# Preparing a weight pair's first blocks ahead of the preceding W1 chunk, and every later run head by seven products, in an fp32 MLP on Trainium2

## The chip, the cores and the metric

The kernel runs on one core of a Trainium2 chip. A core has a matrix engine (PE in the profile, its weight loads PEld), a vector engine (DVE), a scalar engine (ACT), a general engine (POOL) and a sync engine (SP), which here issues the loads of the weights from HBM. Each engine works through its own queue strictly in order and waits on semaphores of the others. Sums of products stand in PSUM, in eight banks of 128 x 512 fp32; everything else stands in SBUF.

The metric is device time of one run in microseconds, the median of several runs. The profile comes from one further run; its span goes from that run's first instruction to its last.

## The reference

A trunk of two layers over 256 tokens of width 2048. Layer 0 mixes with a gated short convolution, layer 1 with multi-head latent attention; both are followed by the same kind of MLP with a hidden width of 8192, which is where the change is:

```python
def sq_relu_mlp(x, w1, w2):
    return jnp.square(jax.nn.relu(x @ w1)) @ w2

for layer in range(DEPTH):          # DEPTH = 2
    ...
    h = layer_norm(ALPHA * h + mix, ln_g[layer, 0], ln_b[layer, 0])
    h = layer_norm(ALPHA * h + sq_relu_mlp(h, mlp_w1[layer], mlp_w2[layer]),
                   ln_g[layer, 1], ln_b[layer, 1])
```

All inputs are float32, 256 tokens are held as two halves of 128, and the result is float32.

## The kernel before

**Split numbers.** Every fp32 operand is cut into a rounded high part and the rest: `split` (L142) has ACT cast `hi` and DVE subtract `lo = src - hi`. A product is then three matrix multiplications, high x high, high x low and low x high (`dot`, L293). So each weight block costs ACT a cast and DVE a subtraction of its full size, besides its time on PE.

**The weight stream.** All weights come in one list, `stream`, in the order of use. An entry is a *unit* (one 128 x 1024 block; two units make one *chunk*, that is 128 columns of W1), or a *pair* of W2 blocks: *plain* or *fast*. `prepare(i)` (L168) loads the raw blocks of an entry into `raws` (6 buffers of 512 KB), and splits them into `hi`/`lo` tiles of `whl` (8 buffers each). It is a generator in one, two or three stages; `take` (L215) runs these stages ahead of the use, up to `WA` = 8 stages past the entry that it hands out.

**Plain and fast groups.** A pair times the activations of two halves is a 2 x 2 block product. A plain group does it with eight products (`PLAINS`, 24 multiplications on PE) on four blocks as they are. A fast group does it with seven (`FAST`, 21 multiplications), after Strassen's and Winograd's manner, and so needs sums of weight blocks. They are made by DVE in place in the raw blocks: three differences (L193, `minus`, 128 x 512 each), each of which touches what the one before it read or wrote, then the split of the two new blocks T1 and T2 (tiles `hi_t`, `lo_t`), a fourth difference and its split T4 (tile `t4`, one buffer). The sums of activation blocks that a fast group needs are made by `forms` (L660) for every chunk pair.

**Order of the work.** `plan` (L81) makes runs of four groups, in turn for the two halves b of the output's columns (the first run has two groups), and puts one chunk of W1 behind each group from the fourth group on. A chunk (L716) is 16 high and 16 low multiplications into one bank `ps_m`, which `whole` (L333) clears with an ACT copy `t` and a DVE addition `sf`; every second chunk is followed by ReLU and square on ACT (L722, L658), `forms` on DVE and a split into `hc` (ACT) and `ha` (DVE). While groups run, `ps_m` has a single bank, so a chunk starts when the `sf` of the chunk before it is done. In `PLAIN` (L39) the pairs 0 and 1 of both halves are plain, and of half 1 also 4, 8, 12, ... 24, the heads of its later runs: ten plain groups of 56 in each layer.

**Turns.** Seven partial sums stand in seven PSUM banks. When a run ends, `Sums.turn` (L604) copies each bank to SBUF (`spill`, L584) and the other half's sum back into it (`seed`, L588), both on ACT. Behind a plain head the sum of product 1 is swapped once more (L741). A scheduler then places all instructions on their engines' queues, by its own estimates; the queue order is what runs.

Of the kernel before, what the change touches and what calls it, by code (L numbers as in the profile page):

```python
# [31 lines left out]
RAW, WA = 6, 8  # L32
# [3 lines left out]
KEPT = PAIRS - QC // 2  # L36
SLOTS = 10
FIRST = ((0, 2, 4, 8), (0, 4, 8))
PLAIN = ((0, 1), (0, 1, *range(4, KEPT, 4)))  # L39
GROUP = 3  # L40
WARM = 8
WO_G = 3
# [6 lines left out]
def trunk(ctx: ExitStack, tc: tile.TileContext, xT, vecs, w_in, w_out, w_kv, w_q, w_uk, w_uv,  # L49
# [26 lines left out]
    stream = []  # L76
# [4 lines left out]
    def plan():  # L81

        nxt, b, steps, m, count = [0, 0], 0, [], QC, 0
        while min(nxt) < KEPT:
            end = min(nxt[b] + (4 if nxt != [0, 0] else 2), KEPT)
            run = [(b, j, j in PLAIN[b]) for j in range(nxt[b], end)]
            for i, (b, j, plain) in enumerate(run):
# [23 lines left out]
    size = {"unit": 1, "plain": 2, "fast": 3}  # L111
    start = [0]
# [3 lines left out]
    class Banks:  # L116
# [15 lines left out]
        @classmethod  # L132
        def next(cls):
            cls.count += 1
            if cls.only is not None:
                return cls.only
            return cls.more if cls.more is not None and cls.count % 8 >= 4 else pmm

    state = {"made": 0, "next": 0}
    ready = {}  # L140

    def split(hi, lo, src):  # L142

        nc.scalar.copy(hi, src)  # L144
        nc.vector.tensor_tensor(lo, src, hi.bitcast(F32), ALU.subtract)  # L145

    def tiled(w):
        return w.rearrange("p (b c) -> p b c", c=P)

    def parts(i):  # L150
        return tuple(whl.tile([P, 8, P], F32R, tag=t, name=f"{t}{i}") for t in ("hi", "lo"))
# [11 lines left out]
    def load_raw(i, src):  # L163
        raw = raws.tile([P, 1024], F32, tag="raw", name=f"raw{i}")
        nc.sync.dma_start(raw, src)
        return raw

    def prepare(i):  # L168

        kind, *src = stream[i]  # L170
        if kind == "unit":
            raw = load_raw(i, src[0])
            hi, lo = ready[i] = parts(i)
            split(hi, lo, tiled(raw))
            yield
            return
        r1, r2 = (load_raw(f"{i}_{j}", v) for j, v in enumerate(src))

        def finished(r, name):
            w = parts(f"{i}_{name}")  # L180
            split(*w, tiled(r))
            return [[v.rearrange("p b c -> p (b c)")[:, o:o + BW] for v in w] for o in (0, BW)]

        b11, b22, b21, b12 = r1[:, :BW], r1[:, BW:], r2[:, :BW], r2[:, BW:]
        out = {}
        if kind == "plain":
            out["11"], out["22"] = finished(r1, 1)
            yield
            out["21"], out["12"] = finished(r2, 2)
            ready[i] = out  # L190
            yield
            return
        minus = lambda o, x, y: nc.vector.tensor_tensor(o, x, y, ALU.subtract)  # L193
        out["11"], out["22"] = finished(r1, 1)
        minus(b11, b12, b11)
        minus(b12, b12, b22)
        minus(b22, b22, b11)
        yield
        out["T1"], out["T2"] = finished(r1, "t")
        minus(b11, b21, b22)  # L200
        f = state["fast"].tile([P, 2, BW], F32R, tag="t4", name=f"t4_{i}", bufs=1)
        split(f[:, 0, :], f[:, 1, :], b11)
        out["T4"] = [f[:, 0, :], f[:, 1, :]]
        yield
        out["21"], out["T3"] = finished(r2, 2)
        ready[i] = out
        yield

    def all_steps():
        for i in range(2 * GROUP, len(stream)):  # L210
            yield from prepare(i)

    making = all_steps()

    def take(n=2):  # L215

        i = state["next"]
        state["next"] += n
        while state["made"] < min(start[i] + WA, start[-1]):
            next(making)  # L220
            state["made"] += 1
        got = [ready.pop(i + j) for j in range(n)]
        return got

    def psum(name):
        return Banks.next().tile([P, 512], F32, tag="mm", name=name)
# [18 lines left out]
    def mm_like(ps, w, x, n=NC):  # L245

        for h in range(0, NC, n):
            for k in range(h, h + n):
                high(ps, w, k, x[k], k == 0)
            for k in range(h, h + n):  # L250
                low(ps, w, k, x[k], k == NC - 1)
# [22 lines left out]
    def group_of(n):  # L274

        return [(take(), psum("ps_g")) for _ in range(n)]
# [56 lines left out]
    def whole(ps, out):  # L333

        t = tmp.tile([P, T], F32, tag="evac", name="t")
        nc.scalar.copy(t, ps[:, T:])
        nc.vector.tensor_tensor(out, ps[:, :T], t, ALU.add)  # L337
# [174 lines left out]
    for half, cuts in enumerate(FIRST):  # L512
        pieces = [load(2 * u + half, first[:, GROUP * half + u, :], cuts) for u in range(GROUP)]
        for b0, b1 in zip(cuts, cuts[1:]):
            at = slice(8 * half + b0, 8 * half + b1)
# [4 lines left out]
                put_split(xhl[m], xres[:, m, :])  # L520
            for p in pieces:
                next(p)
    state["made"] = 2 * GROUP
    nc.sync.dma_start(vec, vecs)

    zt = array("b", F32R, "z", NC, 2 * T)
# [4 lines left out]
    for m in range(NC):  # L531
# [17 lines left out]
        if m >= NC // 2:  # L549
# [4 lines left out]
    summed(ln, products(NC, z), residual)  # L554

    FAST = (("1", "11", "11"), ("3", "S4", "22"), ("5", "S1", "T1"), ("6", "S2", "T2"),
            ("4", "22", "T4"), ("2", "12", "21"), ("7", "S3", "T3"))
    PLAINS = (("3", "12", "22"), ("1", "22", "22"), ("2", "11", "11"), ("4", "21", "11"),
              ("3", "11", "12"), ("1", "21", "12"), ("2", "12", "21"), ("4", "22", "21"))

# [77 lines left out]
    def mlp(idx, ln, hook, blocks, fast):  # L638
# [8 lines left out]
        def normal():  # L647
            k = next(todo, None)
            if k is not None:
                ln.normal(k, xhl[k])  # L650
# [3 lines left out]
        def pair():  # L654
            return fast.tile([P, 8 * P], F32, tag="sf", name="sf", bufs=2)

        def square(f):
            nc.scalar.activation(f[:, :4 * P], f[:, :4 * P], AF.Square)  # L658

        def forms(f):  # L660

            a21, a11, a12 = (f[:, i * P:(i + 1) * P] for i in (1, 0, 2))
            s1, s2, s4 = (f[:, i * P:(i + 1) * P] for i in (4, 6, 7))
            blocks = f.rearrange("p (a c) -> p a c", c=P)
            nc.vector.tensor_tensor(s1, a21, f[:, 3 * P:4 * P], ALU.add)
            nc.vector.tensor_tensor(blocks[:, 5:7, :], blocks[:, 1:5:3, :], a11.unsqueeze(1).to_broadcast([P, 2, P]),
                                    ALU.subtract)
            nc.vector.tensor_tensor(s4, a12, s2, ALU.subtract)
# [31 lines left out]
        def parts_of(j):  # L700

            i = j % 4
            if j >= 4:
                both = [(one[:, i, c * P:(c + 1) * P], two[:, i, c * P:(c + 1) * P]) for c in range(8)]
            else:
                both = [[t[:, i, (4 * o + c) * P:(4 * o + c + 1) * P] for o in range(2)] for t in (one, two) for c in range(4)]
            return dict(zip(NAMES, both))
# [4 lines left out]
        for at, step in enumerate(steps):  # L712
            if step[0] == "m":
                m = step[1]
                w, ps = take(), psum("ps_m")
                mm_like(ps, w, xhl, 8)  # L716
                if m % 2 == 0:
                    f = pair()
                half = f[:, m % 2 * T:(m % 2 + 1) * T]
                whole(ps, half)  # L720
                if m % 2:
                    nc.scalar.activation(f[:, :4 * P], f[:, :4 * P], AF.Relu)  # L722
                    square(f)
                    j, cols = m // 2, 4 * P
                    if j < KEPT:
                        forms(f)
                        cols = 8 * P
                    split(one[:, j % 4, :cols], two[:, j % 4, :cols], f[:, :cols])
                if m == FF // P - 3:
                    Banks.only = None  # L730
                continue
            _, b, j, plain, first, last = step
            w, = take(1)
            later = [s for s in steps[at + 1:] if s[0] == "group"]
            turns = plain and bool(later) and not later[0][3]
            sums.group(b, w, parts_of(j), plain, last, turns)
            if later:
                if last:
                    sums.turn(later[0][1], later[0][3])
                elif turns:  # L740
                    sums.spill("1")  # L741
                    sums.seed("1", (b, "1"))
            if first and j + 4 >= KEPT and b == 0 and j + 2 >= KEPT:
                folded = sums.fold(1)
            if not later:
                folded = sums.combine(0) + folded
            if count < 4:
                normal()
                normal()
            if hook is not None:  # L750
                hook(count)
            count += 1
# [37 lines left out]
    with tc.tile_pool(name="fast1", bufs=1) as fast:  # L790
        mlp(1, before, prepare_one, to_wide, fast)
# [250 lines left out]
    with tc.tile_pool(name="fast2", bufs=1) as fast:  # L1042
        mlp(3, after, None, to_out, fast)
# [86 lines left out]
```

## Time and profile before

| what | value |
|---|---|
| median of 3 runs | 2031.51 us (2030.67 to 2031.93) |
| the profiled run | 2031.37 us |
| span of its profile | 2029.6 us, 29846 instructions |
| granted PE clock, mean | 0.999 |
| first and last multiplication of a group (`sum`) | 413.9 us and 1945.9 us, with the attention layer between |
| loads | 385 MB, 190 GB/s over the span |

Times in the profile are counted from the span's start. In the timeline view a row has the start, the length, the engine, the line, the operation, the tiles written and read, the shape and how many equal instructions stand in the row; in brackets stands how long the engine was idle before it and who ended the wait. Lengths of two instructions in a row overlap a little, so what an instruction costs its engine is read from start to start. Tile names have no numbers there; in queue order listings they have, and the first number is the entry's place in `stream`.

### The profile page before, as it was taken

How to read it: one execution, taken by the hardware profiler on the slowest of the kernel's cores; microseconds unless marked ns; L12 is line 12 of the kernel's file. 1: busy time of each engine (PE TensorE's matmuls, PEld its weight loads, DVE VectorE, ACT ScalarE, POOL GpSimd, SP SyncE). 2: the span in 40 equal slices, each digit the busy share in tenths (PEclk: the TensorE clock that was granted, in tenths of full speed). 3: DMA queues.
4: the chain of work that ended last, by engine and by line, in shares of the span. 5: the costliest groups of instructions: out<-in, count | busy, mean ns of one | idle time of the engine just before them, and what ended most of it. 6: DMA issues, size and time to landing. Idle time of an engine off the chain costs nothing.

```text
span 2029.6 us, 29846 instructions
## 1 busy us (share of the span) xinstructions
PE 2004.9 (99%) x11088; PEld 1735.4 (86%) x11088; DVE 1729.8 (85%) x2575; ACT 1384.2 (68%) x2071; POOL 2.3 (0%) x21
## 2 busy tenths in 40 slices
PE   9999999999999999999999999999999999999997
PEld 8888888988888888888889998898888888888886
DVE  7667677799999999999988888779899999999996
ACT  6444445577877888777756655568777788787861
POOL 0000000000000000000000000000000000000000
PEclk9999999999999999999999999999999999999999
DMA  9665556455555565555654534655555556556672
GB/s 312 206 190 190 189 189 189 150 183 194 180 207 179 205 207 198 203 174 207 235 189 157 167 124 131 201 168 166 187 189 199 193 207 208 182 196 203 207 231 102
DMA packets 108002, 385.31 MB, mean 190 GB/s; under 512 B 11984, under 2 KB 13392, under 8 KB 107856
## 3 DMA queue, kind: packets, MB, share of 16 engines
q1 hardware_dynamic: 107712, 383.13, 56.6%
q8 instruction: 87, 1.43, 0.3%
q14 instruction: 59, 0.48, 0.1%
q10 hardware_dynamic: 144, 0.26, 0.0%
HBM read 381.25 MB, written 2.10 MB: 189 GB/s over the span
## 4 chain that ended last, share of the span: by engine, by line
PE 61%; DVE 17%; ACT 14%; issue 5%; DMA 2%; DVEq 0%; ACTq 0%; SPq 0%
PE ps_u L230 13%; PE ps_m L230 9%; PE ps_u L234 7%; DVE lo L145 7%; PE ps_m L234 5%; DVE raw L193 4%; ACT hi L144 4%; PE sum L296 3%; PE sum L297 3%; PE sum L295 3%; ACT sums L584 2%; ACT hi_t L144 2%; DVE lo_t L145 2%; ACT sum L588 2%; DMA raw<-in_w_dram 1%
## 5 line engine op out<-in xcount | busy, mean ns | idle before, releaser
L145 DVE TENSOR_TENSOR lo<-raw,hi 128x1024 fp32r<-128x1024 f32 x712 | 850.7, 1219 | 127.8 <-ACT hi L144 51.2
L144 ACT CAST hi<-raw 128x1024 fp32r<-128x1024 f32 x712 | 726.2, 1050 | 261.2 <-PE ps_u L230 158.1
L230 PE MATMUL ps_m<-xhl,hi 128*128 128x512 f32 x1792 | 449.3, 391 | 3.0 <-DVE sf L337 2.2
L230 PEld LDWEIGHTS ps_m<-xhl,hi 128*128 128x128 f32 x1792 | 328.6, 188 | 69.1 <-DVE sf L337 2.8
L234 PEld LDWEIGHTS ps_m<-xhl,lo 128*128 128x128 f32 x1792 | 244.3, 190 | 17.4
L234 PE MATMUL ps_m<-xhl,lo 128*128 128x256 f32 x1792 | 249.7, 282 | 0.0
L296 PE MATMUL sum<-lo,hc 128*128 128x512 f32 x512 | 202.9, 396 | 1.0 <-DVE lo L145 1.0
L295 PE MATMUL sum<-hi,hc 128*128 128x512 f32 x512 | 196.8, 396 | 5.2 <-ACT sum L588 5.1
L193 DVE TENSOR_TENSOR raw<-raw,raw 128x512 f32<-128x512 f32 x276 | 189.3, 686 | 3.0
L297 PE MATMUL sum<-hi,ha 128*128 128x512 f32 x448 | 175.1, 391 | 0.0
L144 ACT CAST hi_t<-raw 128x1024 fp32r<-128x1024 f32 x92 | 96.6, 1050 | 113.5 <-DVE raw L193 113.4
L230 PE MATMUL ps_u<-xhl_a,hi 128*128 128x512 f32 x720 | 172.0, 391 | 0.0
L145 DVE TENSOR_TENSOR lo_t<-raw,hi_t 128x1024 fp32r<-128x1024 f32 x92 | 112.7, 1225 | 68.5 <-ACT hi_t L144 68.5
L230 PEld LDWEIGHTS ps_u<-xhl_a,hi 128*128 128x128 f32 x720 | 132.4, 188 | 25.8
L584 ACT COPY sums<-sum 128x512 f32<-128x512 f32 x204 | 118.0, 583 | 43.3 <-PE sum L297 41.4
L295 PEld LDWEIGHTS sum<-hi,hc 128*128 128x128 f32 x512 | 95.6, 188 | 31.5 <-ACT sum L588 9.4
L296 PEld LDWEIGHTS sum<-lo,hc 128*128 128x128 f32 x512 | 96.5, 189 | 23.5 <-DVE lo L145 8.4
L588 ACT COPY sum<-sums 128x512 f32<-128x512 f32 x186 | 110.0, 593 | 2.7
L297 PEld LDWEIGHTS sum<-hi,ha 128*128 128x128 f32 x448 | 84.3, 188 | 15.9
L234 PEld LDWEIGHTS ps_u<-xhl_a,lo 128*128 128x128 f32 x720 | 92.3, 191 | 3.5
L234 PE MATMUL ps_u<-xhl_a,lo 128*128 128x256 f32 x720 | 93.4, 283 | 0.0
L722 ACT ACTIVATE sf<-sf 128x512 f32<-128x512 f32 x56 | 35.4, 631 | 57.2 <-DVE sf L337 57.2
(240 smaller groups left out, 3285.0 us busy)
## 6 DMA issues: line engine op xcount, KB each, us to landing
raw<-in_w_dram SPq DMA_DIRECT2D x288, 512.0 KB, 4.5
raw<-in_w2f_dram SPq DMA_DIRECT2D x224, 512.0 KB, 5.7
raw<-in_w_in_dram SPq DMA_DIRECT2D x90, 512.0 KB, 4.3
raw<-in_w_out_dram SPq DMA_DIRECT2D x32, 512.0 KB, 4.1
raw<-in_w_o_dram SPq DMA_DIRECT2D x32, 512.0 KB, 3.9
raw<-in_w_kv_dram SPq DMA_DIRECT2D x10, 512.0 KB, 4.3
raw<-in_w_q_dram SPq DMA_DIRECT2D x8, 512.0 KB, 4.0
raw<-in_w_uk_dram SPq DMA_DIRECT2D x8, 512.0 KB, 4.2
```

The costliest lines, as they stand in the source:

```text
L144: nc.scalar.copy(hi, src)
L145: nc.vector.tensor_tensor(lo, src, hi.bitcast(F32), ALU.subtract)
L193: minus = lambda o, x, y: nc.vector.tensor_tensor(o, x, y, ALU.subtract)
L230: nc.tensor.matmul(ps, w[blk // 8][0][:, blk % 8, :], x, start=first, stop=False)
L234: nc.tensor.matmul(ps[:, :T], w[blk // 8][1][:, blk % 8, :], x[:, :T], start=False, stop=last)
L295: nc.tensor.matmul(ps, x[0], w[0], start=first, stop=False, skip_group_check=goes_on)
L296: nc.tensor.matmul(ps, x[0], w[1], start=False, stop=False, skip_group_check=goes_on)
L297: nc.tensor.matmul(ps, x[1], w[0], start=False, stop=last, skip_group_check=goes_on)
L584: nc.scalar.copy(self.slot(self.live.pop(p)), self.bank[p])
L588: nc.scalar.copy(self.bank[p], self.at(key))
L722: nc.scalar.activation(f[:, :4 * P], f[:, :4 * P], AF.Relu)
```

## The change

The change has four parts. `PLAIN` loses the heads of later runs, so six more groups of each layer are fast. The stages of `prepare` are ordered anew: wherever the stream has unit, unit, fast, the pair's first stage (both loads, the first split and three differences) now comes ahead of the two units, and its second and third stages behind them; within these, the split of the second raw block changes places with the fourth difference and T4's split. `take` gets a parameter: at a run's last group only five stages ahead are made instead of eight, so that the turn's copies stand ahead of the casts that follow. Last, `FAST` has the product with T4 as the last of its seven instead of the fifth.

```diff
--- before.py
+++ after.py
@@ -36,7 +36,7 @@
 KEPT = PAIRS - QC // 2
 SLOTS = 10
 FIRST = ((0, 2, 4, 8), (0, 4, 8))
-PLAIN = ((0, 1), (0, 1, *range(4, KEPT, 4)))
+PLAIN = ((0, 1), (0, 1))
 GROUP = 3
 WARM = 8
 WO_G = 3
@@ -198,29 +198,41 @@
         yield
         out["T1"], out["T2"] = finished(r1, "t")
         minus(b11, b21, b22)
+        yield
+        out["21"], out["T3"] = finished(r2, 2)
         f = state["fast"].tile([P, 2, BW], F32R, tag="t4", name=f"t4_{i}", bufs=1)
         split(f[:, 0, :], f[:, 1, :], b11)
         out["T4"] = [f[:, 0, :], f[:, 1, :]]
-        yield
-        out["21"], out["T3"] = finished(r2, 2)
         ready[i] = out
         yield
 
-    def all_steps():
-        for i in range(2 * GROUP, len(stream)):
-            yield from prepare(i)
-
-    making = all_steps()
-
-    def take(n=2):
+    sequence, i = [], 2 * GROUP
+    while i < len(stream):
+        if [k for k, *_ in stream[i:i + 3]] == ["unit", "unit", "fast"]:
+            sequence += [i + 2, i, i + 1, i + 2, i + 2]
+            i += 3
+        else:
+            sequence += [i] * size[stream[i][0]]
+            i += 1
+    making = {}
+    last = {i: at for at, i in enumerate(sequence)}
+
+    def make_up_to(n):
+
+        while state["made"] < min(n, len(sequence)):
+            i = sequence[state["made"]]
+            state["made"] += 1
+            if i not in making:
+                making[i] = prepare(i)
+            next(making[i])
+
+    def take(n=2, ahead=None):
 
         i = state["next"]
         state["next"] += n
-        while state["made"] < min(start[i] + WA, start[-1]):
-            next(making)
-            state["made"] += 1
-        got = [ready.pop(i + j) for j in range(n)]
-        return got
+        mine = max(last.get(j, -1) + 1 for j in range(i, i + n))
+        make_up_to(max(mine, start[i] - 2 * GROUP + (WA if ahead is None else ahead)))
+        return [ready.pop(i + j) for j in range(n)]
 
     def psum(name):
         return Banks.next().tile([P, 512], F32, tag="mm", name=name)
@@ -520,7 +532,6 @@
                 put_split(xhl[m], xres[:, m, :])
             for p in pieces:
                 next(p)
-    state["made"] = 2 * GROUP
     nc.sync.dma_start(vec, vecs)
 
     zt = array("b", F32R, "z", NC, 2 * T)
@@ -554,7 +565,7 @@
     summed(ln, products(NC, z), residual)
 
     FAST = (("1", "11", "11"), ("3", "S4", "22"), ("5", "S1", "T1"), ("6", "S2", "T2"),
-            ("4", "22", "T4"), ("2", "12", "21"), ("7", "S3", "T3"))
+            ("2", "12", "21"), ("7", "S3", "T3"), ("4", "22", "T4"))
     PLAINS = (("3", "12", "22"), ("1", "22", "22"), ("2", "11", "11"), ("4", "21", "11"),
               ("3", "11", "12"), ("1", "21", "12"), ("2", "12", "21"), ("4", "22", "21"))
 
@@ -730,7 +741,7 @@
                     Banks.only = None
                 continue
             _, b, j, plain, first, last = step
-            w, = take(1)
+            w, = take(1, 5 if last else None)
             later = [s for s in steps[at + 1:] if s[0] == "group"]
             turns = plain and bool(later) and not later[0][3]
             sums.group(b, w, parts_of(j), plain, last, turns)
```

**DVE, middle of layer 0's MLP, one fast pair (213) and what is made beside it.** `lo213_1` belongs to the pair's first split, the rows L193 on `raw213` are its differences, `lo213_t` T1 and T2, `lo213_2` the second raw block, `t4_213` T4; `lo211` to `lo215` are units of chunks, `sf` clears a chunk, `ha1` belongs to the activations. Before:

```order
L145 TENSOR_TENSOR lo213_1_6367<-raw213_0_6362,hi213_1_6366 128x1024
L337 TENSOR_TENSOR sf_6406<-ps_m_6373,t_6407 128x256
L193 TENSOR_TENSOR raw213_0_6362<-raw213_1_6364,raw213_0_6362 128x512
L193 TENSOR_TENSOR raw213_1_6364<-raw213_1_6364,raw213_0_6362 128x512
L193 TENSOR_TENSOR raw213_0_6362<-raw213_0_6362 128x512
L145 TENSOR_TENSOR lo213_t_6411<-raw213_0_6362,hi213_t_6410 128x1024
L145 TENSOR_TENSOR lo213_2_6419<-raw213_1_6364,hi213_2_6418 128x1024
L193 TENSOR_TENSOR raw213_0_6362<-raw213_1_6364,raw213_0_6362 128x512
L145 TENSOR_TENSOR lo214_6447<-raw214_6444,hi214_6446 128x1024
L145 TENSOR_TENSOR lo215_6453<-raw215_6450,hi215_6452 128x1024
L145 TENSOR_TENSOR t4_213_6415<-raw213_0_6362,t4_213_6415 128x512
L145 TENSOR_TENSOR lo216_1_6461<-raw216_0_6456,hi216_1_6460 128x1024
```

With the change (line numbers are those of the changed file, where L349 is the old L337):

```order
L145 TENSOR_TENSOR lo213_1_6367<-raw213_0_6362,hi213_1_6366 128x1024
L145 TENSOR_TENSOR ha1_4154<-sf_6225,hc1_3517 128x1024
L193 TENSOR_TENSOR raw213_0_6362<-raw213_1_6364,raw213_0_6362 128x512
L145 TENSOR_TENSOR lo211_6376<-raw211_6373,hi211_6375 128x1024
L193 TENSOR_TENSOR raw213_1_6364<-raw213_1_6364,raw213_0_6362 128x512
L145 TENSOR_TENSOR lo212_6382<-raw212_6379,hi212_6381 128x1024
L193 TENSOR_TENSOR raw213_0_6362<-raw213_0_6362 128x512
L349 TENSOR_TENSOR sf_6418<-ps_m_6385,t_6419 128x256
L145 TENSOR_TENSOR lo213_t_6423<-raw213_0_6362,hi213_t_6422 128x1024
L145 TENSOR_TENSOR lo213_2_6428<-raw213_1_6364,hi213_2_6427 128x1024
L193 TENSOR_TENSOR raw213_0_6362<-raw213_1_6364,raw213_0_6362 128x512
L145 TENSOR_TENSOR lo216_1_6461<-raw216_0_6456,hi216_1_6460 128x1024
```

The first three differences stood in a row behind `sf`; now two units' splits stand between them, and behind the third stands `sf`, then `lo213_t`. In place of a plain head 216 (two splits, no differences) the change also has a fast one.

**ACT, the same place, at a turn.** `sums1<-sum5` is a spill, `sum5<-sums1` a seed, L733 and L669 are ReLU and square of a chunk pair, `t` clears a chunk, `hi..._t` is the cast that `lo..._t` waits for. Before, at the turn behind group 225:

```order
L336 COPY t_6894<-ps_m_6861 128x256
L584 COPY sums1_4159<-sum1_4176 128x512
L588 COPY sum1_4176<-sums1_4159 128x512
L584 COPY sums1_4159<-sum3_4172 128x512
L588 COPY sum3_4172<-sums1_4159 128x512
L584 COPY sums1_4159<-sum5_4443 128x512
L722 ACTIVATE sf_6800<-sf_6800 128x512
L588 COPY sum5_4443<-sums1_4159 128x512
L658 ACTIVATE sf_6800<-sf_6800 128x512
L584 COPY sums1_4159<-sum6_4447 128x512
L144 COPY hi228_t_6904<-raw228_0_6850 128x1024
L144 COPY hc1_3517<-sf_6800 128x1024
```

With the change, at the turn behind group 213 (the same twelve rows come again at the turn behind 225):

```order
L348 COPY t_6512<-ps_m_6479 128x256
L595 COPY sums1_4159<-sum5_4443 128x512
L599 COPY sum5_4443<-sums1_4159 128x512
L595 COPY sums1_4159<-sum6_4447 128x512
L599 COPY sum6_4447<-sums1_4159 128x512
L595 COPY sums1_4159<-sum2_4180 128x512
L599 COPY sum2_4180<-sums1_4159 128x512
L733 ACTIVATE sf_6418<-sf_6418 128x512
L595 COPY sums1_4159<-sum7_4454 128x512
L669 ACTIVATE sf_6418<-sf_6418 128x512
L599 COPY sum7_4454<-sums1_4159 128x512
L144 COPY hi216_t_6557<-raw216_0_6456 128x1024
```

Before, the cast `hi228_t` came behind four spills, three seeds, ReLU and square; now `hi216_t` comes behind four spills and four seeds that follow the chunk's `t` in one row, with ReLU and square among the last of them. The casts `hi213_t` to `t4_213` and the copies of sums 1 and 3 stand ahead of these rows.

**SP, the loads.** `raw213_0` and `raw213_1` are a pair's raw blocks, the others units of chunks. Before:

```order
L165 DMA raw211_6350<-in_w1_dram 128x1024
L165 DMA raw212_6356<-in_w1_dram 128x1024
L165 DMA raw213_0_6362<-in_w2f_dram 128x1024
L165 DMA raw213_1_6364<-in_w2f_dram 128x1024
L165 DMA raw214_6444<-in_w1_dram 128x1024
L165 DMA raw215_6450<-in_w1_dram 128x1024
```

With the change:

```order
L165 DMA raw213_0_6362<-in_w2f_dram 128x1024
L165 DMA raw213_1_6364<-in_w2f_dram 128x1024
L165 DMA raw211_6373<-in_w1_dram 128x1024
L165 DMA raw212_6379<-in_w1_dram 128x1024
L165 DMA raw216_0_6456<-in_w2f_dram 128x1024
L165 DMA raw216_1_6458<-in_w2f_dram 128x1024
```

Each pair's two loads moved ahead of the two loads of the chunk that precedes it.

## The prediction

> **What bounds the kernel now.** I read the page first, then busy time by stretch, then PE, DVE and ACT in order of time inside one MLP.
>
> ```profile
> PE 2004.9 (99%) x11088; PEld 1735.4 (86%) x11088; DVE 1729.8 (85%) x2575; ACT 1384.2 (68%) x2071; POOL 2.3 (0%) x21
> ...
> 596.15:681.42 85.27, 84.74 (x429) 70.96 (x428) 78.21 (x98) 68.06 (x97) 0.00 (x0) 1.00 0.59 198
> ...
> 499.95:989.28 489.33, 486.59 (x2456) 407.80 (x2455) 449.91 (x567) 392.46 (x557) 0.00 (x0) 1.00 0.58 198
> 1457.70:1946.96 489.26, 486.36 (x2458) 408.14 (x2458) 449.97 (x567) 392.66 (x557) 0.00 (x0) 1.00 0.58 198
> ```
>
> The stretch 596.15 to 681.42 goes from one plain head's end to the next: eight groups (seven fast, one plain) and eight chunks in 85.27 us, so 42.6 us per run of four. The other two stretches hold, in each layer, the last 46 groups, of which the change turns six: 489.3 us each. PE is busy nearly throughout and DVE for 92%, with clock 1.00. How much PE has to do is read from starts:
>
> ```profile
> 701.96 1.98 PE L230 MATMUL ps_m<-xhl,hi 128*128 128x512 f32 x8
> ...
> 707.51 0.40 PE L295 MATMUL sum<-hi,hc 128*128 128x512 f32 x1
> 707.75 0.40 PE L296 MATMUL sum<-lo,hc 128*128 128x512 f32 x1
> ...
> 712.30 1.98 PE L230 MATMUL ps_m<-xhl,hi 128*128 128x512 f32 x8
> ```
>
> Chunk to chunk is 10.34 us (5.55 the chunk, the rest 21 multiplications at about 0.23). A plain group adds three: 11.03. Eight are 7 x 10.34 + 11.03 = 83.4; measured are 85.27, so PE loses 1.9 per eight, at the turns. PE sets the pace, but see DVE beside it:
>
> ```profile
> 700.71 0.42 DVE L337 TENSOR_TENSOR sf<-ps_m,t 128x256 f32<-128x256 f32 x1
> 701.04 1.41 DVE L193 TENSOR_TENSOR raw<-raw,raw 128x512 f32<-128x512 f32 x2
> 702.48 0.69 DVE L193 TENSOR_TENSOR raw<-raw 128x512 f32<-128x512 f32 x1
> 704.29 1.23 DVE L145 TENSOR_TENSOR lo_t<-raw,hi_t 128x1024 fp32r<-128x1024 f32 x1 [1.11 <-ACT hi_t L144]
> 705.43 1.22 DVE L145 TENSOR_TENSOR lo<-raw,hi 128x1024 fp32r<-128x1024 f32 x1
> 706.57 0.68 DVE L193 TENSOR_TENSOR raw<-raw,raw 128x512 f32<-128x512 f32 x1
> 707.17 2.35 DVE L145 TENSOR_TENSOR lo<-raw,hi 128x1024 fp32r<-128x1024 f32 x2
> 709.44 0.68 DVE L145 TENSOR_TENSOR t<-raw,t 128x512 fp32r<-128x512 f32 x1
> 710.04 1.22 DVE L145 TENSOR_TENSOR lo<-raw,hi 128x1024 fp32r<-128x1024 f32 x1
> 711.18 0.42 DVE L337 TENSOR_TENSOR sf<-ps_m,t 128x256 f32<-128x256 f32 x1
> ...
> 713.57 0.28 DVE L665 TENSOR_TENSOR sf<-sf 128x128 f32<-128x128 f32 x1
> 713.88 0.42 DVE L666 TENSOR_TENSOR sf<-sf 128x256 f32<-128x256 f32 x1
> 714.34 0.29 DVE L668 TENSOR_TENSOR sf<-sf 128x128 f32<-128x128 f32 x1
> 714.84 1.23 DVE L145 TENSOR_TENSOR lo_t<-raw,hi_t 128x1024 fp32r<-128x1024 f32 x1 [0.20 <-ACT hi_t L144]
> ...
> 722.86 0.41 DVE L337 TENSOR_TENSOR sf<-ps_m,t 128x256 f32<-128x256 f32 x1
> ...
> 755.62 0.42 DVE L337 TENSOR_TENSOR sf<-ps_m,t 128x256 f32<-128x256 f32 x1
> ...
> 763.47 0.42 DVE L337 TENSOR_TENSOR sf<-ps_m,t 128x256 f32<-128x256 f32 x1
> ```
>
> From `sf` to `sf` DVE needs 10.47 us for a fast pair without `forms` (700.71 to 711.18), 11.68 with them (to 722.86), so 11.1 on average, more than PE's 10.34. For a plain pair it needs 7.85 (755.62 to 763.47). DVE loses ground over seven fast pairs and wins it back in one plain one. That the lead is used up shows just ahead of a plain group:
>
> ```profile
> 670.54 0.19 PEld L296 LDWEIGHTS sum<-lo,hc 128*128 128x128 f32 x1 [0.18 <-DVE lo L145]
> ```
>
> So DVE is a second bound of the same height, and the plain heads hold it down.
>
> **The change part by part.** *Six heads per layer become fast.* PE loses 12 x 3 multiplications: 36 x 0.227 = 8.2 us in all, and a run of four takes it 41.4. DVE gains per head a split of 128x1024 (1.14 from start to start, 705.43 to 706.57), one of 128x512 (0.60) and four differences, ACT two casts; 24 copies of sums go from ACT. On DVE nothing hides this.
>
> *The order.* From the rows: a 1024 split 1.14, the T4 split 0.60, `sf` 0.33, `forms` 0.31 + 0.46 + 0.21, a difference 0.72 behind another (701.04 to 702.48 for two) but 0.60 with something else behind it (706.57 to 707.17). In the new queue splits stand between the differences, so all four cost 0.60. A fast pair then needs 5 x 1.14 + 0.60 + 0.33 + 4 x 0.60 = 9.03 us; every second has `forms` and `ha` (a 1024 split), 2.12 more. Per run of four: 4 x 9.03 + 2 x 2.12 = **40.4**, still under PE's 41.4.
>
> *The wait that stays.* The third difference, the cast `hi_t`, then `lo_t`: 1.81 us from start to start (702.48 to 704.29). The new queue still puts `lo_t` right behind: in two of four pairs only `sf` stands between (1.81 - 0.60 - 0.33 = 0.88 lost), in one nothing (1.21), in one the three rows of `forms` (0.23). Together **3.2**. The reordering saves dependence gaps, but not this wait.
>
> *The turn.* Now every fourth pair meets ACT's copies:
>
> ```profile
> 703.21 1.05 ACT L144 CAST hi_t<-raw 128x1024 fp32r<-128x1024 f32 x1 [5.03 <-DVE raw L193]
> 704.16 3.90 ACT L144 CAST hi<-raw 128x1024 fp32r<-128x1024 f32 x4
> 707.95 0.62 ACT L144 CAST t<-raw 128x512 fp32r<-128x512 f32 x1
> ...
> 708.74 0.59 ACT L584 COPY sums<-sum 128x512 f32<-128x512 f32 x1
> 709.36 0.59 ACT L588 COPY sum<-sums 128x512 f32<-128x512 f32 x1
> ...
> 711.22 0.59 ACT L584 COPY sums<-sum 128x512 f32<-128x512 f32 x1
> 711.71 0.64 ACT L722 ACTIVATE sf<-sf 128x512 f32<-128x512 f32 x1
> 712.24 0.59 ACT L588 COPY sum<-sums 128x512 f32<-128x512 f32 x1
> 712.75 0.63 ACT L658 ACTIVATE sf<-sf 128x512 f32<-128x512 f32 x1
> 713.28 0.57 ACT L584 COPY sums<-sum 128x512 f32<-128x512 f32 x1
> ```
>
> From one `hi_t` to the next ACT's new queue holds five casts (0.95 each: 4.8), T4's cast (0.52), a seed and `t` (0.9), six copies in a chain (0.62 each: 3.7), then ReLU, copy, square, copy (0.51 each: 2.0): 11.9 us. On DVE, third difference to third difference there is 1.81 + 2 x 1.14 + 0.60 + 2 x 1.14 + 3 x 0.60 + 1.14 + 0.33 = 10.2. The square is wanted by `forms` and the cast by `lo_t`, both next in DVE's queue, so DVE stands for about 1.7; if T1's product runs late and the first spill waits for it, for 2.2. I take **1.9**; below, nothing (ACT was free just before, and the copies could run earlier), above, 2.5.
>
> *The other edits.* T4's product last gives T4 1.4 us more, which moves a lead and no rate. Five stages instead of eight at a turn reorder ACT's queue, counted above. Behind DVE stands PE: a chunk waits for the `sf` of the one before, which waits in DVE's queue behind splits. It shows as PE idle, not as more time.
>
> *The sum.* A run of four: 40.4 + 3.2 + 1.9 = 45.5 us by DVE, against 41.4 by PE: DVE decides, and PE waits about 4. Before it was 42.6, so 2.9 more. Each layer has 11.5 such runs: 11.5 x 45.5 = 523, less 2 for the last chunks, which have no `forms`: 521 against 489.3, 32 more, 64 for both layers. The groups ahead of these are plain or fast as before and end with no lead, as now. The profiled run took 2031.37 (its span of 2029.6 and 1.8 around), close to the median of 2031.51: 2031.4 + 64 = **2095 us**.
>
> **The rivals.** *The copies hide.* If the scheduler's row of copies runs in the 5.03 us that ACT idles ahead of `hi_t` (703.21), the turn costs nothing: 43.6 per run, 1.0 more, 23 x 1.0 - 4 = 19: 2050. For it speaks that ACT is busy for 68.06 of 85.27; against it, that the spills must follow the group's products.
>
> *PE decides.* If the splits between the differences let `hi_t` be ready in time, DVE needs 40.4 and PE sets the pace: 8.2 less, 2023; if the turns' 1.9 per eight go too (5.75 x 2 x 1.9 = 22), 2001. PE's 84.74 of 85.27 speaks for it, the queue with `lo_t` behind the third difference against it. The Trainium skill, "Perfetto Trace Analysis", Identifying the Most-Contended Engine, says to optimise the engine with the highest occupancy first, and that for the matrix engine matmul busy time is no good measure of how near its limit it is; by the first half the 2023 here would be the forecast, and the row of 670.54, where PE waits for DVE, agrees with the second.
>
> *Loads.* A pair's raw blocks are now held across a chunk, and the six buffers come free later.
>
> ```profile
> raw<-in_w_dram SPq DMA_DIRECT2D x288, 512.0 KB, 4.5
> raw<-in_w2f_dram SPq DMA_DIRECT2D x224, 512.0 KB, 5.7
> ```
>
> A load waits for a buffer; in the new queues the split that frees a unit's buffer stands some five microseconds of the DVE rows above ahead of the cast that needs the load, so it just fits. If each of 92 pairs stands 0.4 us for a landing, 37 us more: 2132.
>
> **How the numbers follow.** Forecast 2095 (own range 2071 to 2112, from a turn of 0.9 to 2.7): 0.63. Copies hide, 2050: 0.15. PE decides, 2001 to 2023: 0.13. Loads, 2132: 0.09. The range is 2046 to 2116: it takes in the hidden copies and leaves out PE deciding and most of the loads. A difference under 0.2% (4 us) cannot be told from none. Faster 0.12, the same 0.02, slower 0.86.
>
> **What would show it.** Right: in the stretch of eight groups DVE near 81 us busy of about 91, `lo_t` still waiting for `hi_t` about 0.8 to 1.1 us, chunks (`ps_m`) waiting for `sf`, PE idle some 4 us per run, and one wait of about 2 us for ACT per turn on DVE. Wrong: PE without gaps and chunk starts 10.34 apart (PE decides), no longer wait at a turn (copies hide), or casts that wait for loads. The whole fails if DVE's instructions no longer take 1.14 and 0.60 from start to start.

## The result, and the profile after

The changed kernel takes 2114.01 us (median of 4 runs, 2111.87 to 2114.9) against 2031.72 for the kernel before, run beside it (4 runs, 2030.67 to 2032.4). The ratio is 1.0404, 95% interval 1.0386 to 1.0422: 82 us slower. The forecast was 2095, 64 us slower, with a range up to 2116.

Rows of the page (busy time of the engines; a group's busy time and mean, and the idle time ahead of it; a load's time to landing):

```profile
PE 2017.2 (96%) x11052; PEld 1740.4 (82%) x11052; DVE 1761.8 (83%) x2647; ACT 1397.1 (66%) x2071; POOL 2.3 (0%) x21
...
L242 PE MATMUL ps_m<-xhl,hi 128*128 128x512 f32 x1792 | 465.0, 402 | 77.2 <-DVE sf L349 76.9
...
L145 DVE TENSOR_TENSOR lo_t<-raw,hi_t 128x1024 fp32r<-128x1024 f32 x104 | 127.4, 1225 | 101.9 <-ACT hi_t L144 101.9
...
L595 ACT COPY sums<-sum 128x512 f32<-128x512 f32 x192 | 111.1, 586 | 101.0 <-PE sum L309 98.8
...
raw<-in_w2f_dram SPq DMA_DIRECT2D x224, 512.0 KB, 4.1
```

No engine is at its limit any more. Three engines wait in a ring: VectorE for ScalarE's cast (`lo_t`), PE's chunks for VectorE's `sf`, ScalarE's first spills for PE's products. Loads are not part of it: a w2f load takes 4.1 us from issue to landing, where it took 5.7.

Busy time by stretch (length, then PE, PEld, DVE, ACT, POOL, then the granted clock): eight groups in the middle of a layer, the last 46 groups of each layer, and two runs of four, each from one `lo_t` to the one four pairs later:

```profile
694.97:787.37 92.40, 85.88 (x426) 71.69 (x425) 80.93 (x105) 68.93 (x96) 0.00 (x0) 0.98 0.55 182
499.21:1031.82 532.61, 494.69 (x2438) 411.82 (x2437) 468.35 (x604) 397.47 (x554) 0.00 (x0) 0.98 0.57 182
1499.68:2030.17 530.49, 493.42 (x2443) 411.09 (x2443) 468.02 (x603) 396.99 (x554) 0.00 (x0) 0.98 0.57 183
688.16:733.85 45.69, 42.55 (x216) 35.64 (x215) 40.47 (x52) 34.53 (x49) 0.00 (x0) 1.00 0.56 184
733.85:780.55 46.70, 43.32 (x212) 36.04 (x211) 40.46 (x52) 34.39 (x49) 0.00 (x0) 0.96 0.55 181
```

The two stretches of 46 groups grew from 489.3 to 532.6 and 530.5 us: 84.5 in all, while the spans of the two profiled runs differ by 80.5. So the whole loss lies there, and the rest of the kernel got 4 us shorter. A run takes 45.69 us where the clock stays at 1.00 and 46.70 where it does not; VectorE works 40.5 us in both. Its waits, in order of time:

```profile
699.19 1.22 DVE L145 TENSOR_TENSOR lo_t<-raw,hi_t 128x1024 fp32r<-128x1024 f32 x1 [0.78 <-ACT hi_t L144]
...
709.41 1.23 DVE L145 TENSOR_TENSOR lo_t<-raw,hi_t 128x1024 fp32r<-128x1024 f32 x1 [1.12 <-ACT hi_t L144]
...
721.62 1.23 DVE L145 TENSOR_TENSOR lo_t<-raw,hi_t 128x1024 fp32r<-128x1024 f32 x1 [1.21 <-ACT hi_t L144]
...
732.39 0.29 DVE L676 TENSOR_TENSOR sf<-sf 128x128 f32<-128x128 f32 x1 [1.67 <-ACT sf L669]
...
733.85 1.22 DVE L145 TENSOR_TENSOR lo_t<-raw,hi_t 128x1024 fp32r<-128x1024 f32 x1 [0.38 <-ACT hi_t L144]
...
768.84 1.23 DVE L145 TENSOR_TENSOR lo_t<-raw,hi_t 128x1024 fp32r<-128x1024 f32 x1 [2.75 <-ACT hi_t L144]
...
779.10 0.29 DVE L676 TENSOR_TENSOR sf<-sf 128x128 f32<-128x128 f32 x1 [1.15 <-ACT sf L669]
```

In the first run `lo_t` waits 0.78, 1.12, 1.21 and 0.38 (3.49) and `forms` 1.67 for the square. In the second, the third wait is 2.75 in place of 1.21 and the square's 1.15 in place of 1.67: 1.02 more (its first two waits, not shown here, are 0.78 and 1.12 again). What differs there stands in ScalarE's and PE's rows:

```profile
718.80 0.59 ACT L595 COPY sums<-sum 128x512 f32<-128x512 f32 x1 [3.33 <-PE sum L309]
...
720.53 1.05 ACT L144 CAST hi_t<-raw 128x1024 fp32r<-128x1024 f32 x1
...
730.21 0.59 ACT L599 COPY sum<-sums 128x512 f32<-128x512 f32 x1
730.73 0.63 ACT L733 ACTIVATE sf<-sf 128x512 f32<-128x512 f32 x1
731.26 0.57 ACT L595 COPY sums<-sum 128x512 f32<-128x512 f32 x1
731.73 0.63 ACT L669 ACTIVATE sf<-sf 128x512 f32<-128x512 f32 x1
...
766.03 0.59 ACT L595 COPY sums<-sum 128x512 f32<-128x512 f32 x1 [4.64 <-PE sum L309]
766.65 0.59 ACT L599 COPY sum<-sums 128x512 f32<-128x512 f32 x1
767.27 0.59 ACT L595 COPY sums<-sum 128x512 f32<-128x512 f32 x1
767.76 1.05 ACT L144 CAST hi_t<-raw 128x1024 fp32r<-128x1024 f32 x1
```

```profile
698.46 2.11 PE L242 MATMUL ps_m<-xhl,hi 128*128 128x512 f32 x8 [2.13 <-DVE sf L349]
700.40 1.12 PE L246 MATMUL ps_m<-xhl,lo 128*128 128x256 f32 x8
...
744.15 2.96 PE L242 MATMUL ps_m<-xhl,hi 128*128 128x512 f32 x8 [2.27 <-DVE sf L349]
746.91 1.85 PE L246 MATMUL ps_m<-xhl,lo 128*128 128x256 f32 x8
```

At 720.53 `hi_t` comes behind the turn's first three copies, and at 731.73 the square follows the row of copies that the prediction put there. At 766.03 the first spill waits 4.64 us for PE instead of 3.33, and `hi_t` stands behind it. PE was late because the chunk at 744.15, after 2.27 us idle, ran at half clock: its first eight multiplications took 2.96 us instead of 2.11, the next eight 1.85 instead of 1.12. Such a half-clock stretch stands in 11 of the 23 runs. Ten of these can be set beside undisturbed ones and took 1.0 us more (46.7 against 45.7), which makes 11 us if the eleventh, the last run of its layer, cost as much.

### The profile page after: what moved, and what is told of

Its sections match the earlier page's. It is cut to its first block, busy times and chain, and to the rows that moved or that the text cites. A ratio compares the mean times of both kernels' runs of the same rounds, so it can differ in the third digit from the quotient of the medians.

```text
span 2110.1 us, 29788 instructions
## 1 busy us (share of the span) xinstructions
PE 2017.2 (96%) x11052; PEld 1740.4 (82%) x11052; DVE 1761.8 (83%) x2647; ACT 1397.1 (66%) x2071; POOL 2.3 (0%) x21
## 4 chain that ended last, share of the span: by engine, by line
PE 64%; ACT 17%; DVE 14%; issue 4%; DMA 1%; DVEq 0%; ACTq 0%; SPq 0%
PE ps_u L242 13%; PE ps_m L242 11%; PE ps_u L246 7%; PE ps_m L246 6%; DVE lo L145 5%; ACT hi L144 5%; DVE raw L193 4%; PE sum L309 4%; PE sum L307 4%; PE sum L308 4%; ACT sums L595 3%; ACT sum L599 3%; ACT hi_t L144 2%; PE ps_d L308 1%; PE ps_d L307 1%
## 5 line engine op out<-in xcount | busy, mean ns | idle before, releaser
L242 PE MATMUL ps_m<-xhl,hi 128*128 128x512 f32 x1792 | 465.0, 402 | 77.2 <-DVE sf L349 76.9
L193 DVE TENSOR_TENSOR raw<-raw,raw 128x512 f32<-128x512 f32 x312 | 213.6, 685 | 0.0
L145 DVE TENSOR_TENSOR lo_t<-raw,hi_t 128x1024 fp32r<-128x1024 f32 x104 | 127.4, 1225 | 101.9 <-ACT hi_t L144 101.9
L307 PE MATMUL sum<-hi,hc 128*128 128x512 f32 x464 | 181.1, 391 | 0.0
L308 PE MATMUL sum<-lo,hc 128*128 128x512 f32 x464 | 181.0, 390 | 0.0
L595 ACT COPY sums<-sum 128x512 f32<-128x512 f32 x192 | 111.1, 586 | 101.0 <-PE sum L309 98.8
L144 ACT CAST hi_t<-raw 128x1024 fp32r<-128x1024 f32 x104 | 109.0, 1048 | 94.8 <-DVE raw L193 94.7
L309 PE MATMUL sum<-hi,ha 128*128 128x512 f32 x400 | 156.0, 390 | 0.0
L308 PEld LDWEIGHTS sum<-lo,hc 128*128 128x128 f32 x464 | 87.2, 188 | 17.6
L309 PEld LDWEIGHTS sum<-hi,ha 128*128 128x128 f32 x400 | 75.2, 188 | 14.6
L309 PE MATMUL sum<-hi_t,ha 128*128 128x512 f32 x208 | 80.9, 389 | 0.0
```

Of the source, the lines that this page charges most:

```text
L242: nc.tensor.matmul(ps, w[blk // 8][0][:, blk % 8, :], x, start=first, stop=False)
L307: nc.tensor.matmul(ps, x[0], w[0], start=first, stop=False, skip_group_check=goes_on)
L308: nc.tensor.matmul(ps, x[0], w[1], start=False, stop=False, skip_group_check=goes_on)
L309: nc.tensor.matmul(ps, x[1], w[0], start=False, stop=last, skip_group_check=goes_on)
L595: nc.scalar.copy(self.slot(self.live.pop(p)), self.bank[p])
```

## The experiments

All are timed in 3 rounds beside the kernel before, which took 2030.3 to 2032.0 us there (medians). Every kernel is scheduled anew, so an edit can also move instructions that its diff does not name; where that bears on the reading, it is said. Rows of stretches below have the columns named above.

**The heads alone, in the old queue**

```diff
 (the kernel before)
-PLAIN = ((0, 1), (0, 1, *range(4, KEPT, 4)))
+PLAIN = ((0, 1), (0, 1))
```

> The heads alone: the kernel before with the six plain heads per layer made fast and its old preparation queue. Theory (VectorE's queue decides): a fast pair took VectorE 10.47 us without forms and 11.68 with them, 44.3 us per run of four, and a turn adds 0 to 1.9: 44.3 to 46.2 against 42.6 before, times 23 runs: 2070 to 2114 us. Rival (the loss of the changed kernel sits in its new queue): PE sets the pace and the time is at or under that of before, 2023 to 2035.

2077.62 us, ratio 1.0226 (1.0210 to 1.0241). One run of four:

```profile
648.38:692.82 44.44, 42.92 (x214) 34.88 (x213) 41.18 (x52) 34.17 (x49) 0.00 (x0) 1.00 0.56 189
```

44.44 us, with 2.9 of waits for `hi_t` and none for the square: the row of copies is on ScalarE here too, but VectorE does not reach `forms` before the square is done. So of the 82 us the fast heads alone bring 46, and the new queue (with its five stages and T4's product last), which was to help, adds 36.

**The new queue alone, plain heads kept**

```diff
 (the changed kernel)
-PLAIN = ((0, 1), (0, 1))
+PLAIN = ((0, 1), (0, 1, *range(4, KEPT, 4)))
```

> The new queue alone: the changed kernel with its six plain heads per layer put back. Theory (VectorE decides): eight groups need VectorE 76.6 us of work, about 5.8 of waits for hi_t and 1.7 for the square, 84 in all, against 83.4 of PE's work and 1.9 of stalls at turns: the time comes back to that of before or a little under, 2018 to 2034 us. Rival (the new queue itself costs): most of the 82 us stay, 2080 or more.

2019.81 us, ratio 0.9939 (0.9923 to 0.9956). Eight groups take 83.72:

```profile
646.90:730.62 83.72, 83.72 (x428) 71.36 (x427) 76.90 (x99) 67.44 (x97) 0.00 (x0) 1.00 0.63 203
```

PE has no gap and VectorE works 76.9 of 83.72. The same queue gains 12 us where a plain head in eight groups leaves VectorE room, and costs 36 where none does.

**PE kept at work ahead of the long wait**

```diff
 (the changed kernel; zero is a 128x128 tile of zeros)
                 m = step[1]
+                if at and steps[at - 1][0] == "group" and steps[at - 1][4] and count > 8:
+                    for _ in range(6):
+                        nc.tensor.matmul(sums.bank["4"], zero, xhl[0], start=False, stop=False,
+                                         skip_group_check=True)
```

> The changed kernel with six multiplications by zeros (1.36 us) into sum4 ahead of the second group of a run, where PE stands idle 2.3 to 2.45 us for sf. Theory (PE's clock falls to half behind these idle stretches and makes the next turn late): the idle falls to about 1.1 us, the granted clock stays 1.00, 11 turns lose their 1.02 us: 2103 us. Rival (the slow stretch is cover and costs nothing, or the longer wait at the turn has another cause): 2114 us, within 3.

2102.23 us, ratio 1.0345 (1.0330 to 1.0361): 12 us less. A run now takes what an undisturbed one took, at full clock, though PE does 72 useless multiplications per layer:

```profile
642.35:688.03 45.68, 43.70 (x220) 36.28 (x219) 40.45 (x52) 34.50 (x49) 0.00 (x0) 1.00 0.57 184
```

**One split moved between the third difference and `lo_t`**

```diff
 (the changed kernel)
+        out["21"], out["T3"] = finished(r2, 2)
         out["T1"], out["T2"] = finished(r1, "t")
         minus(b11, b21, b22)
         yield
-        out["21"], out["T3"] = finished(r2, 2)
         f = state["fast"].tile([P, 2, BW], F32R, tag="t4", name=f"t4_{i}", bufs=1)
```

> The changed kernel with the split of a pair's second raw block between the third difference and lo_t, so that the cast hi_t runs beside it. Theory (VectorE's work and its waits for hi_t add up): 2.9 to 3.5 us of 3.5 per run go, a run falls from 45.7 to 42.2 to 42.8 against 41.4 on PE: 2034 to 2047 us. Rival (the turn's copies on ScalarE hold everything, and the waits for hi_t are slack): 2095 or more.

2006.99 us, ratio 0.9884 (0.9870 to 0.9899): 107 us less than the changed kernel and 25 less than the one before. One run of four, and two groups of the page:

```profile
684.83:726.30 41.47, 41.47 (x212) 35.03 (x211) 40.90 (x53) 34.29 (x49) 0.00 (x0) 1.00 0.65 204
```

```profile
L145 DVE TENSOR_TENSOR lo_t<-raw,hi_t 128x1024 fp32r<-128x1024 f32 x104 | 127.0, 1221 | 5.0 <-ACT hi_t L144 4.5
...
L595 ACT COPY sums<-sum 128x512 f32<-128x512 f32 x192 | 111.6, 589 | 1.1 <-PE sum L309 0.6
```

PE decides again, at its floor of 41.4. `lo_t`'s waits fell from 101.9 to 5.0 us and with them went what I had expected to stay: the spills' wait for PE from 98.8 to 0.6, nearly all waits for the square, the half clock. That is the ring seen from the other side: once VectorE's `sf` is in time, PE's products are, and the copies can start early.

One thing besides the moved split changed, though. ScalarE's copies at a turn no longer stand in a row; the scheduler put casts between them, and `hi_t` right behind the first:

```profile
703.48 0.59 ACT L595 COPY sums<-sum 128x512 f32<-128x512 f32 x1 [0.28 <-PE sum L309]
703.96 1.05 ACT L144 CAST hi_t<-raw 128x1024 fp32r<-128x1024 f32 x1
```

How much of the 107 us is due to this order was not separated. The same move in the old queue (below) leaves a row of five copies where it was and still takes the waits for `hi_t` away. (In the change only T4's split had changed places with the split of the second raw block; the fourth difference had stayed in the second stage.)

**Eight stages ahead at a turn**

```diff
 (the changed kernel)
-            w, = take(1, 5 if last else None)
+            w, = take(1)
```

> The changed kernel with eight stages ahead at a turn, as before it, in place of five. At every second and fourth turn VectorE stood 1.67 or 1.15 us for ScalarE's square behind a row of copies, then 0.38 for hi_t. With eight stages the cast hi_t stands ahead of the square, inside the row. Theory (the row of copies itself costs, wherever the cast stands): lo_t is split before forms while the square runs, about 0.5 us per run gone: 2095 to 2106 us. Rival (the number five makes the turn slow): the 1.67 go, 2080 or less. Second rival: nothing hangs on it, 2114.

2091.41 us, ratio 1.0296 (1.0279 to 1.0313): 22 us less than the change, 4 below the theory's range. An undisturbed run takes 44.91 us, 0.78 less (0.5 had been expected), and 7 runs instead of 11 have a half-clock stretch. The five stages were a loss. The row of copies is as long as before, but `hi_t` now stands between ReLU and square:

```profile
727.60 0.63 ACT L733 ACTIVATE sf<-sf 128x512 f32<-128x512 f32 x1
728.13 1.03 ACT L144 CAST hi_t<-raw 128x1024 fp32r<-128x1024 f32 x1
729.07 0.63 ACT L669 ACTIVATE sf<-sf 128x512 f32<-128x512 f32 x1
...
729.20 1.22 DVE L145 TENSOR_TENSOR lo_t<-raw,hi_t 128x1024 fp32r<-128x1024 f32 x1 [1.59 <-ACT hi_t L144]
```

VectorE stands there 1.59 us for `hi_t` and not at all for the square, where it stood 1.67 and 0.38 with five stages.

**The fourth difference on GpSimd**

```diff
 (the changed kernel)
-        minus(b11, b21, b22)
+        nc.gpsimd.tensor_tensor(b11, b21, b22, ALU.subtract)
```

> The changed kernel with the fourth difference of each pair (0.60 us of VectorE's queue) on GpSimd. Theory (VectorE's queue decides): a run loses 4 x 0.60 = 2.4 us, 55 in all, and with PE idle for less the stretches at half clock go too, 11 more: 2048 us, 2040 to 2062. Rival (ScalarE's turn decides, or GpSimd's difference is slow and T4's split stands for it on VectorE): 2090 or more.

2169.33 us, ratio 1.0680 (1.0664 to 1.0696): 55 us more, where 66 less were expected. Two runs of four, VectorE's two splits and GpSimd's difference beside them, and VectorE's group that was hit most:

```profile
648.75:696.90 48.15, 44.45 (x214) 36.29 (x213) 42.62 (x49) 34.63 (x49) 6.89 (x4) 0.96 0.56 173
696.90:745.05 48.15, 43.17 (x214) 35.04 (x213) 42.62 (x48) 34.51 (x49) 6.90 (x4) 1.00 0.56 176
```

```profile
663.67 3.44 DVE L145 TENSOR_TENSOR lo<-raw,hi 128x1024 fp32r<-128x1024 f32 x2
...
663.88 2.15 POOL L200 TENSOR_TENSOR raw<-raw,raw 128x512 f32<-128x512 f32 x1 [12.48 <-DVE lo_t L145]
...
674.38 2.25 DVE L145 TENSOR_TENSOR lo<-raw,hi 128x1024 fp32r<-128x1024 f32 x1 [0.25 <-ACT hi L144]
```

A difference of 0.60 left VectorE's queue and its busy time rose from 40.5 to 42.6 us per run. The split at 674.38 takes 2.25 us instead of 1.22 while GpSimd works; GpSimd needs 1.3 or 2.15 for what took VectorE 0.68. This run refutes the expectation, not the bound: VectorE's queue got longer, and so did the time. The half-clock stretches stayed as well, but here they cost nothing: of the two runs above one holds such a stretch and the other none, and both take 48.15 us. The Trainium skill, "SBUF — State Buffer", Who interferes with whom, says that a VectorE operation on two SBUF tensors contends with GpSimd's reads; the rows agree.

**The old queue with the split moved**

```diff
 (the kernel of the first experiment)
+        out["21"], out["T3"] = finished(r2, 2)
         out["T1"], out["T2"] = finished(r1, "t")
         minus(b11, b21, b22)
+        yield
         f = state["fast"].tile([P, 2, BW], F32R, tag="t4", name=f"t4_{i}", bufs=1)
...
         out["T4"] = [f[:, 0, :], f[:, 1, :]]
-        yield
-        out["21"], out["T3"] = finished(r2, 2)
```

> The old queue with fast heads (measured at 2077.6 us, 44.44 us per run with 2.88 of waits for hi_t) and the split of the second raw block put between the third difference and lo_t. Theory (work plus waits of VectorE): 41.6 us per run against PE's 41.4: 2011 to 2018 us, with the old queue as well. Rival (only the new queue lets the waits go): 2035 or more.

2020.84 us, ratio 0.9953 (0.9938 to 0.9968): 57 us less than with the heads alone. A run takes 42.15 us instead of 41.6 (a split now waits 0.39 for its own cast in every second pair), hence the miss by 3 us of the range.

**T4's product fifth again**

```diff
 (the changed kernel)
-            ("2", "12", "21"), ("7", "S3", "T3"), ("4", "22", "T4"))
+            ("4", "22", "T4"), ("2", "12", "21"), ("7", "S3", "T3"))
```

> The changed kernel with the product of T4 fifth, as before it, in place of last. The prediction said that this moves a lead and no rate: 2108 to 2118 us. Rival (the late product makes the turn's row of copies late, from which the waits for the square come): 2080 or less. Second rival (T4's place was a gain): PE waits for T4 at each group, 2125 or more.

2114.66 us, ratio 1.0412 (1.0397 to 1.0428). Nothing hangs on it.

**A turn without its seeds**

```diff
 (the changed kernel)
             if key in self.store:
-                nc.scalar.copy(self.bank[p], self.at(key))
                 self.drop(key)
```

> The changed kernel without the copies that read sums back into PSUM at a turn: seven of a turn's fourteen copies are left out, and the sums of two halves mix. Theory (the row of copies on ScalarE keeps the square, and with it forms, waiting): the row falls from 3.7 us to about 2.5 and ReLU, hi_t and the square follow at once; of the 2.05 us per run that VectorE stood for the square and hi_t there 1.2 stay: 2080 to 2095 us. Rival (the row is late because PE's products are, and its length does not matter): 2105 or more.

2071.96 us, ratio 1.0200 (1.0183 to 1.0217): 42 us less, below the range. A run takes 44.43 us, without a wait for the square and without a half-clock stretch, but this does not show that the row's length is what matters, since here too the scheduler put `hi_t` between ReLU and square:

```profile
677.91 1.04 ACT L144 CAST hi_t<-raw 128x1024 fp32r<-128x1024 f32 x1
...
678.99 1.23 DVE L145 TENSOR_TENSOR lo_t<-raw,hi_t 128x1024 fp32r<-128x1024 f32 x1 [1.57 <-ACT hi_t L144]
```

VectorE stands 1.57 us there, hardly less than the 1.59 behind the full row with eight stages. So in both kernels in which the cast stands ahead of the square the wait for the square is gone, whether the row is long or short. What the shorter row does take away is 0.43 us at the turn's first copies: `lo_t` waits 0.78 there instead of 1.21. The range was missed because 1.2 us per run and the slow clock had been left in.

**The split moved in the kernel before, and plain heads in the fastest kernel**

The first has the diff of the old queue above, with plain heads; the second is the kernel with the split moved and `PLAIN` as before the change.

> The kernel before, plain heads and old queue, with the second raw block's split between the third difference and lo_t alone. Theory (before, VectorE had no lead left by the time of a turn, and PE lost 1.9 us per eight groups there): VectorE gains 2.9 us of 45 per run, PE decides and the stalls go: 2008 to 2018 us. Rival (PE's stalls before came from the turn's copies alone): 2025 or more.

> The fastest kernel so far (e4_swap, 2007 us) with the six plain heads per layer put back. Theory (PE decides in both): 36 multiplications more at 0.227 us: 8.2 us more, 2012 to 2018 us. Rival (the plain heads still help through VectorE): 2007 or less.

2010.77 us, ratio 0.9899 (0.9885 to 0.9914), and 2011.86 us, ratio 0.9902 (0.9887 to 0.9917), just under its range. In both PE has no gap; eight groups of the second:

```profile
644.90:728.57 83.67, 83.67 (x429) 71.29 (x428) 77.50 (x99) 68.47 (x97) 0.00 (x0) 1.00 0.65 202
```

So the stalls that the kernel before had at its turns went too, as VectorE's waits for `hi_t` did (5.6 us per eight groups before, 0.7 in the first kernel here). With PE as the bound the fast heads are worth 4.9 us between medians (2011.86 to 2006.99) where 8.2 were expected; the intervals of the two ratios overlap, so the size stays open.

Side by side (medians in us):

| | old queue | new queue |
|---|---|---|
| plain heads | 2031.7 | 2019.8 |
| fast heads | 2077.6 | 2114.0 |
| plain heads, split moved | 2010.8 | 2011.9 |
| fast heads, split moved | 2020.8 | 2007.0 |

The moved split alone takes 21 us from the kernel before. Fast heads and new queue on top of it bring 4 more, and the intervals of these two ratios overlap too.

## Why the prediction was right, and where it was too low

*VectorE decides, PE waits.* Right. In the old queue with fast heads the moved split took 2.1 us of VectorE's waits from a run and 2.3 us from its length; in the changed kernel, where it also came with a new order of ScalarE's copies, it took 107 us in all. PE, with 41.4 us per run, did not set the pace in the changed kernel.

*40.4 us of work per run.* Measured 40.5.

*The wait that stays, 3.2.* Measured 3.49: 0.78, 1.12, 1.21 and 0.38 where 0.88 twice, 1.21 and 0.23 were taken. Most of it is the third difference, the cast, and `lo_t` right behind, as the moved split shows by removing it. But the pairs do not match one by one: where nothing stands between, 1.12 were lost (at 709.41), and the 1.21 stand where `sf` does, 0.78 for the cast and 0.43 for the turn's first copies ahead of it. Without these 0.43 the term is 3.1; that 3.2 came so close to 3.49 is in part luck.

*The turn, 1.9.* Measured 1.67 for the square, which did stand behind the row of copies, and the 0.43 above: 2.1. The prediction got its 1.7 from the length of ScalarE's queue. That step is not shown: with `hi_t` ahead of the square the wait for the square went with a full row as well as with a halved one, and 1.6 us for `hi_t` stayed in both. Since an undisturbed run took 45.7 us against 45.5, the three terms account for 0.2 x 23 = 5 of the 18 us by which the forecast was low.

*Where it failed.* The step reads: "It shows as PE idle, not as more time." PE's idle time did become more time. An idle stretch of 2.3 us can halve PE's clock for 3.4 us, the products of the next turn come late, and a spill that waits for them holds `hi_t` up: 1.02 us in 11 runs, 11 us. The zeros that only keep PE busy took 12 us away. Together that is 16 us. The books do not close, though: the two stretches grew by 20 us more than the 64 forecast, so some 5 are left there, and the rest of the kernel got 4 us shorter, which was not forecast. The last run of each layer has a part in the 5: it took 48.6 and 47.1 us, with 43.8 of work on VectorE in place of 40.5. Neither was followed up. The time lies 2 us above the 2112 up to which the mechanism's own range went and 2 us below the end of the stated range, 2116, which was drawn wider for the rivals and not for the slow clock; that it was met is luck too.

*The rivals.* Copies that hide: they do in the old queue with fast heads (no wait for the square, 44.44 us), not in the new one. PE decides: only once the wait for `hi_t` is gone; then the time is 2007, inside the 2001 to 2023 that the rival gave. The rule of the Trainium skill cited there, "Perfetto Trace Analysis", Identifying the Most-Contended Engine, in its first half would have had the change gain because PE was at 99%; the runs go against that half. They do not need its second half: eight groups of the kernel before took 85.27 us, and 83.62 without a gap on PE once the split was moved, so PE was near its limit, and VectorE was as well. Loads: a w2f load took less time to land than before, and no cast of the eight groups waited for one.

*Not in the prediction.* It did not say what the queue's order is worth by itself. Going by the two kernels with eight stages at a turn (fast heads in the old and in the new queue, 1.0226 and 1.0296 of before), the new sequence costs 14 us: it takes VectorE's work from 41.5 to 40.2 us per run and its waits from 2.9 to 4.7. The five stages cost another 22.

## What to carry to other kernels

When two engines stand at the same height, cost a change on both before trusting the busier one, and price an engine's queue as work plus dependence waits: here 40.5 us of work did not fit under 41.4 because 5 us of waits came with it. A wait of difference, cast, subtraction is best filled with independent work that is already in the queue: one split moved there gained 21 us in the kernel before, and heads and queue on top of it 4, with intervals that overlap. An idle stretch on an engine is not always free just because another engine sets the pace: where three engines wait for each other in a ring, it cost 1 us a time here, and in the kernel with GpSimd nothing.

## What the runs showed of the hardware

**PE's clock is set for stretches of 3.41 us on a fixed grid, and about 1.9 us of idle time inside one stretch halves the next.** Five stretches of the changed kernel (length, PE busy, ..., then the granted clock):

```profile
693.95:697.36 3.41, 2.38 (x11) 1.65 (x9) 3.41 (x5) 0.71 (x2) 0.00 (x0) 1.00 0.77 252
697.36:700.77 3.41, 2.31 (x12) 1.98 (x13) 2.63 (x5) 2.66 (x3) 0.00 (x0) 1.00 0.84 306
741.74:745.15 3.41, 1.14 (x5) 0.86 (x5) 2.63 (x5) 1.35 (x2) 0.00 (x0) 1.00 0.79 286
745.15:748.56 3.41, 3.41 (x13) 2.97 (x12) 3.41 (x4) 3.41 (x5) 0.00 (x0) 0.50 0.37 150
748.56:751.97 3.41, 3.41 (x21) 3.00 (x20) 3.41 (x5) 0.97 (x3) 0.00 (x0) 1.00 0.66 173
```

The wait of 2.13 us at 698.46 falls on two stretches, about 1.0 us in each, and costs nothing; the one of 2.27 at 744.15 lies in a single stretch, and the next runs at 0.50. The 11 slow stretches in the runs of this trace begin whole multiples of 3.413 us apart (the one at 745.15 is the 54th behind the one at 560.83), and the stretch ahead of each had at least 1.88 us idle; between 100 and 2000 us no other stretch had more than 1.70. The border is no sharper than that: 1.85 us idle halved the clock in the kernel with eight stages (510.68 to 514.09) and did not in the one with GpSimd (706.40 to 709.81). So in the changed kernel the same wait is free or costs 1 us by where it falls. The Trainium skill, "TensorE: Matmul & The Clock Gate", Part 1, The HAM clock gate, gives the stretch as about 3.4 us, free-running, which agrees; it has the clock fall after a whole idle stretch, and here little more than half of one was enough.

**GpSimd was no spare engine beside VectorE here.** 1.3 to 2.15 us of GpSimd's difference stretched a VectorE split by about 1 us, more than the 0.60 it was to save.
